# A recurrent weighted average in chunks: v cast to bf16 by its load, constant matrices built on another engine, and the last steps of the state placed anew

## The chip, the cores and the metric

The kernel runs on one core of one Trainium2 chip. The metric is the device time of one execution in microseconds. The names of the engines are those of the profile: PE is the matmul engine, DVE the vector engine, ACT the scalar engine (exponentials, logarithms), POOL the GpSimd engine, SP the engine that issues transfers. POOL and SP both have a queue of transfers between HBM and the on-chip memory (SBUF); all transfers run on the same 16 DMA engines.

## The reference

`k` and `v` are 16 sequences of 2048 steps with 256 channels, `w` and `u` one vector of 256 each, all f32. Each sequence and channel keeps a weighted sum of v (`aa`) and of weights (`bb`), with a running exponent `pp` that keeps the exponentials in range:

```python
for t in range(seq_len):
    ww = u + kk                       # kk, vv: row t of k and v
    qq = np.maximum(pp, ww)
    e1, e2 = np.exp(pp - qq), np.exp(ww - qq)
    output[b, t] = (e1 * aa + e2 * vv) / (e1 * bb + e2 + 1e-08)
    ww = pp - w + kk
    qq = np.maximum(ww, kk)
    e1, e2 = np.exp(ww - qq), np.exp(kk - qq)
    aa, bb, pp = e1 * aa + e2 * vv, e1 * bb + e2, qq
```

## The kernel before, in words

Time is cut into a head of 32 steps and 16 steps of time of 126 rows each. Rows of time lie on the 128 partitions. For one step of time the 16 sequences are taken four at a time, which gives four *pairs* (two tiles of two sequences, 512 columns each). With two pairs for the heads there are 66 pairs, and the main loop runs over them by number `n`, with a tail of 12 rounds (`for n in range(NP + LAG + 2)`).

A pair goes through these steps; line numbers are those of the profile before.

- `load(n)`, four pairs ahead (`AHEAD = 4`): one transfer of k and one of v, 512 KB each, both f32 (L135; for the heads L129). The first two pairs and the heads' k are issued by SP, everything else by POOL.
- `round_k(n)` (L285, DVE): k into the type the matmul reads.
- `logs(n)` (L301, PE): two constant matrices turn k into the exponents of the weights, in PSUM.
- `exps(n)` (L315, L317, ACT): the exponentials, bf16, into the buffer `ez`.
- `cast_v(n)` (L328 on DVE; L326 on ACT for pairs 2 to 7): v into bf16, buffer `vb`.
- `times_v(n)` (L336, DVE): the weights times v, bf16, also into `ez`.
- `sums(n)` (L366, PE): sums over time for the state.
- ten rounds later (`LAG = 10`; six for the heads): `den` (L512, PE) the denominators, `log_den` and `invert` (L521, L526, ACT) their reciprocals as exp of minus the logarithm, `num` (L534, PE) the numerators, `mult` (L542, DVE) the product, and `store` (L562; heads L553), issued by POOL.

Once per step of time a chain of small operations carries the state: `copy_sums`, `turn_sums` (L382), `split_sums` (L389), the state's logarithms and weights (L401 to L421), `state_sums` to `state_decay` (L439 to L450), `inject_logs`, `inject_weights` (L455, L461), `carry_weights`, `carries` (L466, L473), `turn_carries` (L479) and `inject` (L484), whose four small transfers on SP (L488) put the carried state as two more rows into `ez`, where `den` and `num` read them.

Nothing is left to a scheduler: a helper `K` pins every engine's instructions to the order in which the program writes them. The small operations are put into slots of the main loop by tables (`PLANS`): an entry such as `(2, "d3", state_offset, 0)` means the slot `d3` of the round two after the step's last pair. There are plans for the head, the first step, all steady steps and the last.

The constant matrices that `den` and `num` read (`Id`, `IdN`, `It`, `Lh`, `LhN`, `Lf`, `LfN`) are built by POOL in rounds 3, 4 and 5 (L253 to L273), between its transfers.

Of the kernel before, what the change touches and what calls it, by code (L numbers as in the profile page):

```python
# [7 lines left out]
F32 = mybir.dt.float32  # L8
# [14 lines left out]
def kernel(  # L23
# [28 lines left out]
    HS = 63  # L52
# [7 lines left out]
    AHEAD = 4  # L60
    LAG = 10
    HALVES = 8

    SHARED = range(2, HALVES)
    RS = 2.0 ** -43
    LNRS = 43 * 0.6931471805599453
    CAP = 68.0
# [2 lines left out]
    consts = ctx.enter_context(tc.tile_pool(name="consts", bufs=1))  # L70
    kpool = ctx.enter_context(tc.tile_pool(name="kpool", bufs=AHEAD))
    vpool = ctx.enter_context(tc.tile_pool(name="vpool", bufs=AHEAD))
    vbpool = ctx.enter_context(tc.tile_pool(name="vbpool", bufs=2))
# [25 lines left out]
    def is_head(n):  # L99
        return pairs[n][0] < 0  # L100
# [5 lines left out]
    def tiles_of(n):  # L106
        return 1 if pairs[n] == (-1, 1) else 2
# [5 lines left out]

    def load(n):
        kr = kpool.tile([128, 4, Dm], F32, tag="kr", name="kr")
        vr = vpool.tile([128, 4, Dm], F32, tag="vr", name="vr")
        kr_of[n], vr_of[n] = kr, vr
        c, p = pairs[n]
        if is_head(n):
            if p == 1:  # L120
                K(POOL.memset(kr[64:96, 0:2, :], 0.0))
                K(POOL.memset(vr[64:96, 0:2, :], 0.0))

            for t, x, eng, groups in ((kr, k, SP, range(NG)), (vr, v, POOL, reversed(range(NG)))):
                for g in groups:
                    b = 6 * g + 4 * p
                    e = min(b + 2 * tiles_of(n), B)
                    if b < e:
                        K(eng.dma_start(out=t[g * GB:(g + 1) * GB, 0:e - b, :],  # L129
                                        in_=x[b:e, 0:T0, :].rearrange("n t d -> t n d")))  # L130
        else:
            t0 = T0 + c * TC
            r = min(128, T - t0)
            for t, x in ((kr, k), (vr, v)):
                K((SP if n < 2 else POOL).dma_start(  # L135
                    out=t[0:r, :, :], in_=x[4 * p:4 * p + 4, t0:t0 + r, :].rearrange("n t d -> t n d")))


    crow = consts.tile([128, Dm], F32, tag="crow", name="crow")
# [12 lines left out]
    def matrix(name, dt, width=128):  # L152
        return consts.tile([128, width], dt, tag=name, name=name)
# [3 lines left out]
    def select(ap, cmp, fill, base, cm, n, step):  # L157
        K(POOL.affine_select(out=ap, in_=ap, pattern=[[step, n]], compare_op=cmp,
                             fill=fill, base=base, channel_multiplier=cm))
# [21 lines left out]
    K(POOL.memset(cc[:, 5:6], CAP - LNRS))  # L181
    select(cc[:, 4:5], GE, 0.0, -HS, 1, 1, 0)
    select(cc[:, 4:5], GE, 0.0, TC - 1, -1, 1, 0)

    def head_blocks(f):
        fill(f[0:GB, GB:NH], 0.0)
# [63 lines left out]

    def matrices_for_outputs():

        K(POOL.tensor_copy(It, I1))  # L253
        K(POOL.tensor_copy(Id, I1))
        K(POOL.tensor_copy(Id[:, TC:128], I1[:, TC - 1:TC].broadcast_to([128, 128 - TC])))
        K(POOL.tensor_scalar(IdN, Id, RS, None, ALU.mult))

    def matrices_for_outputs_of_head():
        for t, s in ((Lh, 1.0), (LhN, RS)):
            K(POOL.tensor_scalar(t, M1, -s, None, ALU.mult))  # L260
            K(POOL.memset(t[0:GB, GB:NH], 0.0))
            K(POOL.memset(t[GB:2 * GB, 2 * GB:NH], 0.0))
            K(POOL.memset(t[:, NH:128], 0.0))

    def more_matrices_for_outputs():
        Lx = matrix("Lx", F32)
        K(POOL.tensor_scalar(Lx, M1, -1.0, None, ALU.mult))
        K(POOL.memset(Lx[0:HS, HS:TC], 0.0))
        K(POOL.tensor_scalar(Lx[:, 0:HS], Lx[:, 0:HS], cc[:, 2:3], None, ALU.add))
        K(POOL.tensor_scalar(Lx[:, HS:TC], Lx[:, HS:TC], cc[:, 3:4], None, ALU.add))  # L270
        K(POOL.tensor_copy(Lx[:, TC:128], Lx[:, TC - 1:TC].broadcast_to([128, 128 - TC])))
        K(POOL.tensor_copy(Lf, Lx))
        K(POOL.tensor_scalar(LfN, Lx, RS, None, ALU.mult))  # L273


    EZ, X_of, KM = {}, {}, {}
# [39 lines left out]
        else:  # L316
            K(SC.activation(ez_of(n)[:, 0:4:2], X[2][:, :, 0:i, :], ACT.Exp))  # L317

    VB = {}

    def cast_v(n):
        r = NH if is_head(n) else TC
        i = 2 * tiles_of(n)
        vb = vbpool.tile([128, 4, Dm], BF16, tag="vb", name="vb")
        if n in SHARED:
            K(SC.activation(vb[0:r, 0:i, :], vr_of.pop(n)[0:r, 0:i, :], ACT.Copy))  # L326
        else:
            K(DVE.tensor_copy(vb[0:r, 0:i, :], vr_of.pop(n)[0:r, 0:i, :]))  # L328
        VB[n] = vb

    def times_v(n):
        ez = ez_of(n)
        i = tiles_of(n)
        r = NH if is_head(n) else TC
        vb = VB.pop(n).rearrange("p (i n) d -> p i (n d)", i=2)
        K(DVE.tensor_mul(ez[0:r, 1:4:2], ez[0:r, 0:4:2],  # L336
                         vb[0:r, 0:i, :].unsqueeze(1).broadcast_to([r, 2, i, D])))

# [205 lines left out]
    def store(n):  # L544
        o = RD.pop(n).rearrange("p i (n d) -> p (i n) d", n=2)
        if n % 2 == 1:
            EZ.pop(n // 2)
        if is_head(n):
            for g in range(NG):
                b = 6 * g + 4 * pairs[n][1]  # L550
                e = min(b + 2 * tiles_of(n), B)
                if b < e:
                    K(POOL.dma_start(out=out[b:e, 0:T0, :].rearrange("n t d -> t n d"),  # L553
                                     in_=o[g * GB:(g + 1) * GB, 0:e - b, :]))
        else:
            c, p = pairs[n]
            t0 = T0 + c * TC


            r = rows_of(n)  # L560
            for a, b, eng in ((0, 2, POOL), (2, 4, SP)) if n == NP - 1 else ((0, 4, POOL),):
                K(eng.dma_start(out=out[4 * p + a:4 * p + b, t0:t0 + r, :].rearrange("n t d -> t n d"),  # L562
                                 in_=o[0:r, a:b, :]))

# [9 lines left out]
    def small_work(n, where):  # L574
        for f, args in later.pop((n, where), []):
# [14 lines left out]
                   (3, "d4", state_decay, 0), (4, "a0", inject_logs), (4, "a2", inject_weights),  # L590
                   (4, "d4", carry_weights), (4, "d5", carries), (4, "p4", turn_carries), (5, "d0", inject),
                   (5, "d2", state_add, 1), (5, "d4", state_decay, 1)),
        "last": ((1, "a0", copy_sums), (1, "p1", turn_sums), (1, "p1", split_sums), (1, "a2", state_logs),
                 (1, "d5", state_offset, 0), (1, "d5", state_offset, 1), (1, "d5", state_near),
                 (1, "a1", state_weights), (2, "d0", state_sums), (2, "d0", state_add, 0),
                 (2, "d0", state_decay, 0), (2, "a2", inject_logs), (2, "a2", inject_weights),
                 (2, "d2", carry_weights), (2, "d2", carries), (2, "p2", turn_carries), (2, "d5", inject)),
    }
    for c in range(-1, NST):
        for slot, where, f, *args in PLANS["head" if c < 0 else "first" if c == 0 else  # L600
                                           "last" if c + 1 == NST else "steady"]:
# [6 lines left out]
    matrices_for_sums()  # L608
    round_k(0)
    logs(0)  # L610
    cast_v(0)

    out_at = {n + (LAG - 4 if is_head(n) else LAG): n for n in range(NP)}
    for n in range(NP + LAG + 2):

        q, qi, qp = out_at.get(n), out_at.get(n - 1), out_at.get(n - 2)
        live, more, out_q, out_qi, out_qp = n < NP, n + 1 < NP, q is not None, qi is not None, qp is not None
        if n == NP:
            widen()
        if n + AHEAD < NP:  # L620
            load(n + AHEAD)
        small_work(n, "a3")
        if live:
            exps(n)
        small_work(n, "d0")
        if more:
            round_k(n + 1)
        small_work(n, "p0")
        if out_qp:
            num(qp, 0)  # L630
            if not live:
                num(qp, 1)
        small_work(n, "d1")
        small_work(n, "a0")
        small_work(n, "p1")
        if out_qi and qi < NP - 1:
            invert(qi)
        small_work(n, "a2")
        if out_q:
            den(q)  # L640
            if q < NP - 1:
                log_den(q)
            else:
                for i in range(2):
                    log_den(q, i, i + 1)
                    invert(q, i, i + 1)
        if out_qp:
            mult(qp, 0)
        small_work(n, "d2")
        if more:  # L650
            cast_v(n + 1)
# [49 lines left out]
```

## Time and profile before

| what | value |
|---|---|
| median of 13 runs | 325.17 us (322.6 to 331.73) |
| the profiled execution's own time | 325.17 us |
| its span in the profile | 323.5 us |
| PE, DVE, ACT busy | 279.4, 277.4, 278.1 us (86% each) |
| POOL busy | 179.4 us (55%) |
| HBM read, written | 68.12 MB, 34.05 MB |

The profile lists, for each engine, when it was busy, and for each idle stretch what ended it. A stage table (stretch in us, busy time of PE, weight loads, DVE, ACT, POOL, granted clock, share of time in which the 16 DMA engines had a packet in work, GB/s) shows where in the span an engine is full. Packets of one DMA engine overlap by a little, so the share can read above 1. In a row of the groups stand the line, the engine, the operation, the shapes, the count, the total and mean duration, and the idle time ahead of it with its cause.

### The profile page before, as it was taken

Reading aid. Unit: us, or ns where it says so; the run is one execution under the profiler, and the core shown is the slowest. Engines: PE = TensorE matmul, PEld = TensorE weight load, DVE = VectorE, ACT = ScalarE, POOL = GpSimd, SP = SyncE. Lnnn points to the kernel's source line nnn. Section 1 sums busy time; section 2 is a strip of 40 time slices with the busy share of each in tenths; the row PEclk is TensorE's granted clock in tenths of the full one; section 3 lists DMA queues with packets and bytes.
Section 4 is the critical chain, followed back from the end, with each engine's and each line's share of the span. In section 5 each row is a group of like instructions: output and inputs, shape, how many; then the busy total and the mean of one; then the engine's idle time right before and its main releaser. Section 6 shows DMA issues by size and latency. Waiting matters only on the chain. (4 is left out here: it accounts for less than half of the span.)

```text
span 323.5 us, 3974 instructions
## 1 busy us (share of the span) xinstructions
PE 279.4 (86%) x1132; PEld 126.0 (39%) x1132; DVE 277.4 (86%) x546; ACT 278.1 (86%) x318; POOL 179.4 (55%) x249
## 2 busy tenths in 40 slices
PE   2589679889999999999999999999999999987970
PEld 1134334344444444444434444443444444433420
DVE  4565887989999999999999999999999999987670
ACT  6468888789899998989898989999898989796990
POOL 8669954673665555666464666555566656122331
PEclk9999999999999999999999999999999999999995
DMA  6999699999999999999999999999999999944875
GB/s 199 224 326 300 201 316 317 320 324 337 331 353 335 364 375 370 358 367 366 360 356 365 370 361 367 359 364 354 365 370 358 357 317 295 302 177 135 295 253 166
DMA packets 33743, 102.96 MB, mean 318 GB/s; under 512 B 6638, under 2 KB 9482, under 8 KB 33722
## 3 DMA queue, kind: packets, MB, share of 16 engines
q0 software_dynamic: 27616, 99.27, 90.0%
q1 hardware_dynamic: 6074, 3.42, 4.4%
q8 instruction: 9, 0.15, 0.2%
q14 instruction: 12, 0.10, 0.1%
q10 hardware_dynamic: 32, 0.02, 0.1%
HBM read 68.12 MB, written 34.05 MB: 316 GB/s over the span
## 5 line engine op out<-in xcount | busy, mean ns | idle before, releaser
L562 POOL DMA_DIRECT2D out_dram<-rd x64 | 53.7, 840 | 120.5 <-issue 43.0
L317 ACT ACTIVATE ez<-X 128x2048 bf16<-128x2048 f32 x58 | 108.7, 1873 | 8.2 <-PE num L534 6.3
L542 DVE TENSOR_TENSOR rd<-num,rd 128x512 f32<-128x512 f32 (+2 forms) x131 | 88.8, 684 | 14.1 <-ACT rd L526 6.7
L336 DVE TENSOR_TENSOR ez<-ez,vb 126x2048 bf16<-126x2048 bf16 (+1 forms) x66 | 79.7, 1207 | 7.2 <-ACT ez L315 6.8
L521 ACT ACTIVATE rd<-den 128x1024 f32<-128x1024 f32 (+3 forms) x67 | 66.9, 998 | 15.4 <-PE den L512 13.4
L526 ACT ACTIVATE rd<-rd 128x1024 f32<-128x1024 f32 (+3 forms) x67 | 69.4, 1035 | 0.3
L301 PE MATMUL X<-km,NLE 128*128 128x512 f32 x128 | 52.3, 490 | 11.0 <-DVE km L285 8.6
L135 POOL DMA_DIRECT2D kr<-in_k_dram x62 | 56.1, 905 | 2.8 <-DVE kmh L285 1.6
L534 PE MATMUL num<-ez,LfN 128*128 128x512 bf16 x128 | 49.1, 384 | 4.4 <-DVE rd L542 0.8
L135 POOL DMA_DIRECT2D vr<-in_v_dram x62 | 48.6, 784 | 4.7 <-DVE ez L336 2.9
L534 PE MATMUL num<-ez,IdN 126*128 126x512 bf16 (+1 forms) x131 | 49.8, 380 | 0.0
L328 DVE CAST vb<-vr 126x1024 bf16<-126x1024 f32 x60 | 46.3, 772 | 1.0 <-DMA vr<-in_v_dram 1.0
L285 DVE CAST km<-kr 126x1024 fp32r<-126x1024 f32 x64 | 44.2, 691 | 2.8 <-ACT ez L315 1.9
L366 PE MATMUL tot<-ez,OHV 126*48 126x512 bf16 x128 | 38.9, 385 | 8.7 <-DVE ez L336 7.3
L301 PE MATMUL X<-km,NLZ 128*128 128x512 f32 x128 | 41.4, 405 | 0.3 <-ACT ez L315 0.2
L366 PE MATMUL tot<-ez,OHE 128*48 128x512 bf16 x128 | 40.1, 396 | 0.0
L512 PE MATMUL den<-ez,Lf 128*128 128x512 bf16 x128 | 38.0, 378 | 2.1 <-DMA ez<-row 1.3
L512 PE MATMUL den<-ez,Id 126*128 126x512 bf16 (+1 forms) x131 | 39.1, 378 | 0.0
L301 PEld LDWEIGHTS X<-km,NLE 128*128 128x128 f32 x128 | 23.9, 194 | 23.7 <-DVE km L285 6.5
L301 PEld LDWEIGHTS X<-km,NLZ 128*128 128x128 f32 x128 | 24.7, 194 | 6.8 <-ACT ez L315 1.2
L366 PEld LDWEIGHTS <-OHV 126*48 126x48 bf16 x128 | 13.4, 104 | 31.2 <-issue 22.3
L534 PEld LDWEIGHTS <-LfN 128*128 128x128 bf16 x128 | 12.3, 96 | 28.6 <-issue 25.4
(111 smaller groups left out, 215.8 us busy)
## 6 DMA issues: line engine op xcount, KB each, us to landing
out_dram<-rd POOLq DMA_DIRECT2D x60, 512.0 KB, 7.2
kr<-in_k_dram POOLq DMA_DIRECT2D x58, 512.0 KB, 8.1
vr<-in_v_dram POOLq DMA_DIRECT2D x58, 512.0 KB, 8.6
kr<-in_k_dram POOLq DMA_DIRECT2D x4, 504.0 KB, 11.2
vr<-in_v_dram POOLq DMA_DIRECT2D x4, 504.0 KB, 12.1
out_dram<-rd POOLq DMA_DIRECT2D x3, 504.0 KB, 4.4
kr<-in_k_dram SPq DMA_DIRECT2D x2, 512.0 KB, 5.4
vr<-in_v_dram SPq DMA_DIRECT2D x2, 512.0 KB, 9.5
```

Of the source, the lines that this page charges most:

```text
L135: K((SP if n < 2 else POOL).dma_start(out=t[0:r, :, :], in_=x[4 * p:4 * p + 4, t0:t0 + r, :].rearrange("n t d -> t n d")))
L301: K(PE.matmul(X[q][:, i, :], m[0:kr, :], km[0:kr, i, :], start=True, stop=True))
L317: K(SC.activation(ez_of(n)[:, 0:4:2], X[2][:, :, 0:i, :], ACT.Exp))
L328: K(DVE.tensor_copy(vb[0:r, 0:i, :], vr_of.pop(n)[0:r, 0:i, :]))
L336: K(DVE.tensor_mul(ez[0:r, 1:4:2], ez[0:r, 0:4:2], vb[0:r, 0:i, :].unsqueeze(1).broadcast_to([r, 2, i, D])))
L366: K(PE.matmul(TOT[c], m[0:r, :], ez_of(n)[0:r, q, i, :], start=n == first_of[c] and i == 0 and q == 0, stop=n == last_of[c] and i == tiles ...
L512: K(PE.matmul(d[:, i, :], m[0:r, :], ez_of(n)[0:r, q, i, :], start=q == 0, stop=q == 2, skip_group_check=True))
L521: K(SC.activation(RD[n][0:r, a:b, :], DEN[n][0:r, a:b, :], ACT.Ln, scale=RS))
L526: K(SC.activation(RD[n][0:r, a:b, :], RD[n][0:r, a:b, :], ACT.Exp, scale=-1.0))
L534: K(PE.matmul(d, m[0:r, :], ez_of(n)[0:r, q, i, :], start=q == 1, stop=q == 3, skip_group_check=True))
L542: K(DVE.tensor_mul(RD[n][0:r, i, :], NUM.pop((n, i))[0:r, :], RD[n][0:r, i, :]))
L562: K(eng.dma_start(out=out[4 * p + a:4 * p + b, t0:t0 + r, :].rearrange("n t d -> t n d"), in_=o[0:r, a:b, :]))
```

## The change

Five things are edited.

1. v is loaded into a bf16 buffer, so the transfer casts; `cast_v` and the buffer `vb` are gone, and `times_v` reads the loaded buffer. POOL issues all of these loads: the first two pairs' v loads move from SP to POOL, behind the first of POOL's constants. The heads' v groups are issued in rising order.
2. The output matrices are built by DVE, in the same slots, with `LhN` and `LfN` made from `Lh` and `Lf`.
3. The state chain of the last step but one gets a plan of its own, `"before"`: most of its entries stand between a few slots and a whole round earlier than in the steady plan. The chain of the last step has some entries in other slots.
4. In the tail, one pair's second numerator is issued a little later, and one pair's denominators a round earlier, ahead of the last carries.
5. The last store but one is issued by SP.

```diff
-        vr = vpool.tile([128, 4, Dm], F32, tag="vr", name="vr")
+        vr = vpool.tile([128, 4, Dm], BF16, tag="vr", name="vr")
...
-            for t, x, eng, groups in ((kr, k, SP, range(NG)), (vr, v, POOL, reversed(range(NG)))):
-                for g in groups:
+            for t, x, eng in ((kr, k, SP), (vr, v, POOL)):
+                for g in range(NG):
...
-            for t, x in ((kr, k), (vr, v)):
-                K((SP if n < 2 else POOL).dma_start(
-                    out=t[0:r, :, :], in_=x[4 * p:4 * p + 4, t0:t0 + r, :].rearrange("n t d -> t n d")))
+            K((SP if n < 2 else POOL).dma_start(
+                out=kr[0:r, :, :], in_=k[4 * p:4 * p + 4, t0:t0 + r, :].rearrange("n t d -> t n d")))
+            if n >= 2:
+                load_v(n)
+
+    def load_v(n):
...
+        K(POOL.dma_start(out=vr_of[n][0:r, :, :],
+                         in_=v[4 * p:4 * p + 4, t0:t0 + r, :].rearrange("n t d -> t n d")))
...
     select(cc[:, 4:5], GE, 0.0, TC - 1, -1, 1, 0)
+    for n in range(2):
+        load_v(n)
...
-        K(POOL.tensor_copy(It, I1))
-        K(POOL.tensor_copy(Id, I1))
-        K(POOL.tensor_copy(Id[:, TC:128], I1[:, TC - 1:TC].broadcast_to([128, 128 - TC])))
-        K(POOL.tensor_scalar(IdN, Id, RS, None, ALU.mult))
+        K(DVE.tensor_copy(It, I1))
+        K(DVE.tensor_copy(Id[:, 0:TC], I1[:, 0:TC]))
+        K(DVE.tensor_copy(Id[:, TC:128], I1[:, TC - 1:TC].broadcast_to([128, 128 - TC])))
+        K(DVE.tensor_single_scalar(IdN, Id, RS, op=ALU.mult))
...
-        for t, s in ((Lh, 1.0), (LhN, RS)):
-            K(POOL.tensor_scalar(t, M1, -s, None, ALU.mult))
...
+        K(DVE.tensor_single_scalar(Lh, M1, -1.0, op=ALU.mult))
+        head_blocks(Lh)
+        fill(Lh[:, NH:128], 0.0)
+        K(DVE.tensor_single_scalar(LhN, Lh, RS, op=ALU.mult))
...
-    def cast_v(n):
...
-        vb = VB.pop(n).rearrange("p (i n) d -> p i (n d)", i=2)
+        vb = vr_of.pop(n)[:, 0:2 * i, :].rearrange("p (i n) d -> p i (n d)", n=2)
...
-            for a, b, eng in ((0, 2, POOL), (2, 4, SP)) if n == NP - 1 else ((0, 4, POOL),):
+            for a, b, eng in ((0, 2, POOL), (2, 4, SP)) if n == NP - 1 else ((0, 4, SP if n == NP - 2 else POOL),):
...
+        "before": ((1, "a0", copy_sums), (1, "p2", turn_sums), (1, "d5", split_sums), (2, "a3", state_logs),
+                   (2, "d1", state_offset, 0), (2, "d2", state_offset, 1), (2, "d3", state_near),
+                   (2, "a1", state_weights), (3, "d0", state_sums), (3, "d1", state_add, 0),
+                   (3, "d1", state_decay, 0), (3, "a0", inject_logs), (3, "a2", inject_weights),
+                   (3, "d4", carry_weights), (3, "d5", carries), (3, "p4", turn_carries), (4, "d0", inject),
+                   (4, "d2", state_add, 1), (4, "d4", state_decay, 1)),
...
-                 (1, "d5", state_offset, 0), (1, "d5", state_offset, 1), (1, "d5", state_near),
+                 (1, "d2", state_offset, 0), (1, "d2", state_offset, 1), (1, "d2", state_near),
...
-                 (2, "d2", carry_weights), (2, "d2", carries), (2, "p2", turn_carries), (2, "d5", inject)),
+                 (2, "d5", carry_weights), (2, "d5", carries), (2, "a1", turn_carries), (2, "a1", inject)),
...
-            if not live:
+            if n > NP:
                 num(qp, 1)
...
+        if n == NP:
+            num(qp, 1)
...
-            den(q)
+            if q not in DEN:
+                den(q)
+            if n == NP + 1:
+                den(q + 1)
```

More of the change, by code (lines that the diff above doesn't have):

```diff
@@ L62 @@
     HALVES = 8
-    SHARED = range(2, HALVES)
     RS = 2.0 ** -43
@@ L72 @@
     vpool = ctx.enter_context(tc.tile_pool(name="vpool", bufs=AHEAD))
-    vbpool = ctx.enter_context(tc.tile_pool(name="vbpool", bufs=2))
     ezpool = ctx.enter_context(tc.tile_pool(name="ezpool", bufs=7))
@@ L133, in load @@
             r = min(128, T - t0)
-            for t, x in ((kr, k), (vr, v)):
-                K((SP if n < 2 else POOL).dma_start(
-                    out=t[0:r, :, :], in_=x[4 * p:4 * p + 4, t0:t0 + r, :].rearrange("n t d -> t n d")))
+            K((SP if n < 2 else POOL).dma_start(
[3 more added lines that the diff above has]
+    def load_v(n):
+        c, p = pairs[n]
+        t0 = T0 + c * TC
+        r = min(128, T - t0)
+        K(POOL.dma_start(out=vr_of[n][0:r, :, :],
+                         in_=v[4 * p:4 * p + 4, t0:t0 + r, :].rearrange("n t d -> t n d")))
     crow = consts.tile([128, Dm], F32, tag="crow", name="crow")
@@ L251, in matrices_for_outputs @@
     def matrices_for_outputs():
-        K(POOL.tensor_copy(It, I1))
-        K(POOL.tensor_copy(Id, I1))
-        K(POOL.tensor_copy(Id[:, TC:128], I1[:, TC - 1:TC].broadcast_to([128, 128 - TC])))
-        K(POOL.tensor_scalar(IdN, Id, RS, None, ALU.mult))
+        K(DVE.tensor_copy(It, I1))
+        K(DVE.tensor_copy(Id[:, 0:TC], I1[:, 0:TC]))
+        K(DVE.tensor_copy(Id[:, TC:128], I1[:, TC - 1:TC].broadcast_to([128, 128 - TC])))
+        K(DVE.tensor_single_scalar(IdN, Id, RS, op=ALU.mult))
     def matrices_for_outputs_of_head():
-        for t, s in ((Lh, 1.0), (LhN, RS)):
[L260 to L263, printed above, removed]
-    def more_matrices_for_outputs():
[L266 to L273, printed above, removed]
+        K(DVE.tensor_single_scalar(Lh, M1, -1.0, op=ALU.mult))
+        head_blocks(Lh)
+        fill(Lh[:, NH:128], 0.0)
+        K(DVE.tensor_single_scalar(LhN, Lh, RS, op=ALU.mult))
+    def more_matrices_for_outputs():
+        K(DVE.tensor_single_scalar(Lf, M1, -1.0, op=ALU.mult))
+        fill(Lf[0:HS, HS:TC], 0.0)
+        K(DVE.tensor_scalar(Lf[:, 0:HS], Lf[:, 0:HS], cc[:, 2:3], None, ALU.add))
+        K(DVE.tensor_scalar(Lf[:, HS:TC], Lf[:, HS:TC], cc[:, 3:4], None, ALU.add))
+        K(DVE.tensor_copy(Lf[:, TC:128], Lf[:, TC - 1:TC].broadcast_to([128, 128 - TC])))
+        K(DVE.tensor_single_scalar(LfN, Lf, RS, op=ALU.mult))
     EZ, X_of, KM = {}, {}, {}
@@ L317, in exps @@
             K(SC.activation(ez_of(n)[:, 0:4:2], X[2][:, :, 0:i, :], ACT.Exp))
-    VB = {}
-    def cast_v(n):
[L322 to L329, printed above, removed]
     def times_v(n):
@@ L334, in times_v @@
         r = NH if is_head(n) else TC
-        vb = VB.pop(n).rearrange("p (i n) d -> p i (n d)", i=2)
+        vb = vr_of.pop(n)[:, 0:2 * i, :].rearrange("p (i n) d -> p i (n d)", n=2)
         K(DVE.tensor_mul(ez[0:r, 1:4:2], ez[0:r, 0:4:2],
-                         vb[0:r, 0:i, :].unsqueeze(1).broadcast_to([r, 2, i, D])))
+                         vb[0:r].unsqueeze(1).broadcast_to([r, 2, i, D])))
     TOT, SUMS = {}, {}
@@ L600 @@
         for slot, where, f, *args in PLANS["head" if c < 0 else "first" if c == 0 else
-                                           "last" if c + 1 == NST else "steady"]:
+                                           "last" if c + 1 == NST else "before" if c + 2 == NST else "steady"]:
             at(last_of[c] + slot, where, f, c, *args)
@@ L610 @@
     logs(0)
-    cast_v(0)
     out_at = {n + (LAG - 4 if is_head(n) else LAG): n for n in range(NP)}
@@ L649 @@
         small_work(n, "d2")
-        if more:
-            cast_v(n + 1)
         small_work(n, "d3")
```

## The prediction

> **What bounds the kernel now.** I read the first part of the page, then the busy time by stage, the waits of each engine inside the steady stretch, and last the account of the DMA queues.
>
> ```profile
> span 323.5 us, 3974 instructions
> PE 279.4 (86%) x1132; PEld 126.0 (39%) x1132; DVE 277.4 (86%) x546; ACT 278.1 (86%) x318; POOL 179.4 (55%) x249
> ...
> 20.00:30.00 10.00, 10.00 (x29) 4.15 (x27) 5.32 (x7) 7.66 (x11) 8.07 (x15) 1.00 1.03 348
> 30.00:40.00 10.00, 7.38 (x28) 3.17 (x27) 8.00 (x17) 8.89 (x16) 9.41 (x15) 1.00 0.62 190
> 40.00:50.00 10.00, 7.75 (x33) 3.46 (x32) 8.50 (x14) 7.99 (x9) 4.78 (x6) 1.00 1.03 320
> 50.00:60.00 10.00, 9.05 (x38) 4.01 (x37) 8.03 (x16) 9.50 (x10) 6.52 (x9) 1.00 0.97 295
> 60.00:100.00 40.00, 36.59 (x152) 16.88 (x152) 37.23 (x73) 35.13 (x41) 22.65 (x27) 1.00 1.00 341
> 100.00:260.00 160.00, 150.66 (x632) 68.71 (x631) 153.73 (x295) 148.27 (x166) 93.08 (x110) 1.00 1.02 362
> ```
>
> The columns after the stretch are PE, weight loads, DVE, ACT, POOL, then the granted clock, the DMA engines' busy share and GB/s. Three engines tie at 86% over the span. From 100 to 260 us DVE is the fullest, 153.73 of 160 us (96%), PE has 94% and ACT 93%. The last but one column is as important: 1.02. The packets of one DMA engine overlap a little, so "always busy" is not 1.00; where loads alone queue up (20 to 30 us) it reads 1.03. So beside a DVE at 96% stand DMA engines at about 1.02 / 1.03 = 99%.
>
> ```profile
> 149.45 1.88 ACT L317 ACTIVATE ez<-X 128x2048 bf16<-128x2048 f32 x1 [0.24 <-PE num L534]
> 166.88 1.88 ACT L317 ACTIVATE ez<-X 128x2048 bf16<-128x2048 f32 x1 [0.22 <-PE num L534]
> ...
> DVE row L484 <- PE den L479: 3.9, 12, 0.3
> PE tot L366 <- DVE ez L336: 5.0, 13, 0.8
> ACT rd L521 <- PE den L512: 9.0, 12, 1.4
> ```
>
> Between those two exponentials lies one step of time of four pairs: 17.43 us, 4.36 us a pair. The three waits are the longest of DVE, PE and ACT from 60 to 260 us (total, times, longest): all on each other, none on a load. So an in-order round of the compute engines sets the pace, DVE first in it, and the DMA engines just keep up, with no slack to speak of.
>
> **The change, part by part.**
>
> *The casts of v.* They go from DVE and ACT.
>
> ```profile
> L328 DVE CAST vb<-vr 126x1024 bf16<-126x1024 f32 x60 | 46.3, 772 | 1.0 <-DMA vr<-in_v_dram 1.0
> 60.00:260.00 200.00, 36.28 (x46) 1.00 1.02 358
> L326 ACT ACTIVATE vb<-vr 126x1024 bf16<-126x1024 f32 x4 | 4.2, 1057 | 0.0
> ```
>
> The middle row is L328 alone: 36.28 / 46 = 0.79 us a pair, 3.16 us a step. DVE would fall from 16.75 us a step (153.73 / 160 x 17.43) to 13.6. The next floors are PE, 150.66 / 160 x 17.43 = 16.4 us, and ACT, 16.2 us. If nothing else bound, a step would take about 16.4 us, 1.0 less. The DMA engines come first: at 1.03 in place of 1.02 a step takes 17.43 x 1.02 / 1.03 = 17.26 us. So most of what DVE gives up becomes idle time of DVE, if a casting load costs the DMA engines what a plain one does.
>
> *The price of a casting load* is the open question: no run shows one. It reads the same f32 bytes from HBM and writes half as many into SBUF. What 16 engines charge for a plain megabyte (queue, kind: packets, MB, share of 16 engines):
>
> ```profile
> q0 software_dynamic: 764, 2.79, 103.0%
> ...
> q0 software_dynamic: 796, 2.92, 84.4%
> ...
> q0 software_dynamic: 3950, 14.39, 100.0%
> ...
> q0 software_dynamic: 1556, 5.27, 102.1%
> ```
>
> These are the stretches 22 to 30 us (loads alone), 302 to 312 (stores alone), 140 to 180 (the steady mix) and 262 to 280. Share x length x 16 / MB gives 47.3, 46.2, 44.5 and 55.8 engine-us per MB. A load (512 KB, 0.524 MB) is then 0.524 x 44.5 / 16 = 1.46 us of all engines, three transfers 4.37 us: the pair's 4.36 again. Loads and stores alone cost nearly the same, so I find no sign that the write into SBUF is dearer than the read, and take an unchanged price, 44.5. Lower end: priced by the bytes written, half of it. Upper end: the dearest row, 55.8, and beyond it two passes, 89. The v loads are 64 x 0.524 + 0.45 = 34 MB, so each engine-us per MB is worth 34 / 16 = 2.1 us of run time while the DMA engines are full.
>
> The Trainium skill, page "Collectives: The Full Stack", Part 3 (why ReduceScatter is half of AllGather), says that the ALU inside a DMA engine adds no cycles and that the number of reads sets the rate; by it the price would be the unchanged one. No run here shows it yet. Its page "DMA: Bandwidth & Descriptors", section Bandwidth, speaks against any steady gain: HBM gives a core about 358 GB/s. By that, 12 x 0.524 MB take 17.6 us a step, no less than now, and the sum below would lose its 2.7 us and end near 320. The row below is this case's answer.
>
> ```profile
> 108.00:120.00 12.00, 11.16 (x48) 4.95 (x46) 11.53 (x23) 11.76 (x15) 7.88 (x9) 1.00 1.03 377
> ```
>
> 377 GB/s over 12 us lies above that limit, so I keep 1.03 as the mark.
>
> *The steady sum.* Filling 1.00 and 1.02 up to 1.03 is worth 40 x 0.03 / 1.03 + 160 x 0.01 / 1.03 = 2.7 us. From 262 to 280 us one queue alone takes 102.1%, so nothing is to be had there.
>
> *The new wait.* The v buffer is now freed by the product (L336), not the cast, and POOL's load of v four pairs on waits for it.
>
> ```profile
> 152.87 0.83 POOL L135 DMA_DIRECT2D vr<-in_v_dram  x1
> 153.32 1.21 DVE L336 TENSOR_TENSOR ez<-ez,vb 126x2048 bf16<-126x2048 bf16 x1
> 154.58 0.68 DVE L542 TENSOR_TENSOR rd<-num,rd 128x512 f32<-128x512 f32 x1
> 155.83 0.77 POOL L562 DMA_DIRECT2D out_dram<-rd  x1 [2.13 <-ACT ez L317]
> ```
>
> The load moves from 152.87 to about 154.53. Behind it on POOL is the store, which needs the product at 154.58 to 155.26 anyway and was issued at 155.83; a load of about 0.8 us fits before that, at most 0.2 us late, and the consumer also moved from the cast to L336. Price 0, bound 0.2 us a pair where POOL is late, nothing while stores are not awaited.
>
> *Constants from POOL to DVE.*
>
> ```profile
> 27.49 2.02 POOL L260 TENSOR_SCALAR LhN<-M 128x128 bf16<-128x128 f32 x1
> ...
> 31.23 0.75 POOL L135 DMA_DIRECT2D vr<-in_v_dram  x1
> 32.01 0.97 POOL L267 TENSOR_SCALAR Lx<-M 128x128 f32<-128x128 f32 x1
> ...
> 36.06 0.53 POOL L273 TENSOR_SCALAR LfN<-Lx 128x128 bf16<-128x128 f32 x1
> 36.55 1.01 POOL L135 DMA_DIRECT2D kr<-in_k_dram  x1
> ...
> L484 DVE CAST row<-den 128x128 bf16<-128x128 f32 x15 | 4.4, 291 | 4.5 <-PE den L479 4.5
> ```
>
> Between 32.0 and 36.6 us POOL builds Lx, Lf and LfN while loads queue behind; the DMA share of 30 to 40 us is 0.62. That hole is 10 x 0.41 / 1.03 = 4.0 us of DMA time, and 50 to 60 us holds another 0.6. On DVE there are 15 instructions, at most 0.29 us each by the L484 row: 4.4 us as an upper bound, beside 10 - 5.32 + 10 - 8.00 = 6.7 us of idle DVE from 20 to 40 us. Cost 0 while that cover lasts, 4.4 us without it. ACT loses its casts of 1.06 us each between the early exponentials, so these follow each other sooner and buffers free earlier. Since a load also waits for its buffer, I count 3.6 of the 4.6 us; the ends are 0 and 4.6.
>
> *The start.* The first two v loads leave SP and follow POOL's first constants; the heads' k loads move up on SP, POOL's later loads move back by two issues.
>
> ```profile
> 2.36 0.51 SPq L135 DMA_DIRECT2D vr<-in_v_dram  x1
> 2.71 0.89 POOL L158 TENSOR_SCALAR_AFFINE_SELECT cc<-cc 128x1 f32<-128x1 f32 x4
> ...
> 12.99 0.69 DVE L328 CAST vb<-vr 126x1024 bf16<-126x1024 f32 x1 [0.26 <-DMA vr<-in_v_dram]
> 13.60 1.22 DVE L336 TENSOR_TENSOR ez<-ez,vb 126x2048 bf16<-126x2048 bf16 x1
> ...
> 16.59 0.69 DVE L285 CAST kmh<-kr 96x1024 fp32r<-96x1024 f32 x1 [1.77 <-DMA kr<-in_k_dram]
> ```
>
> The issue moves from 2.36 to 3.60 at the earliest. The first product ran only at 13.60, behind the cast of the second v at 12.99; that order is gone. At 16.59 DVE waits for a head's k, which now has two 0.51 us issues fewer ahead of it on SP (1.0 us), while POOL's loads 2 and 3 come 1.5 us later (two issues at 0.75). I take 0, ends -1.5 and +1.5.
>
> *The tail.* ACT's waits after 283 us:
>
> ```profile
> ACT rd L521 <- PE den L512: 1.1, 2, 0.7
> ACT lf L401 <- DVE tsum L389: 0.9, 1, 0.9
> ACT w L420 <- DVE near L410: 0.6, 1, 0.6
> ACT rd L521 <- DMA out_dram<-rd: 0.4, 1, 0.4
> ```
>
> 3.0 us idle, the rest of the tail is logarithm and exponential back to back on ACT. The plan that starts the last but one chain a pair earlier, the last chain's new places and the denominators ahead of the carries work on these; I count half, 1.5 us, ends +1 (a chain misplaced) and -3.0. The last but one store on SP leaves POOL's queue: 0.
>
> **Sum.** -2.7 - 3.6 + 0 - 1.5 = -7.8 us. The profiled execution took 325.17 us, 1.7 beside its span, and is itself the median of the 13 runs. 325.2 - 7.8 = 317.4: I say 317.5.
>
> **The rivals.**
>
> *The compute floor.* If the cast makes the load cheaper, priced by bytes written, the DMA engines drop to five sixths and PE's 16.4 us a step binds: 1.0 us for each of the 12.6 steps from 42 to 262 us, 12.6 in place of 2.7. 325.2 - 12.6 - 3.6 - 1.5 = 307.5. For it: DVE's 96% and the waits among compute engines. Against it: the near equal loads and stores above.
>
> *The casting load is dearer: slower.* The DMA engines become the bound with less throughput, every k and v load comes late and DVE waits for them. The gain of 7.8 us is used up at 7.8 / 2.1 = 3.7 engine-us per MB, a price of 48.2 (8% more); from about 49 on the kernel is slower. At 55.8 it is 11.3 x 2.1 = 24 us: 317.5 + 24 = 341. At two passes, 44.5 x 2.1 = 93: 411. For it: DMA at 99% leaves no cover at all. Against it: the read side, which is unchanged.
>
> *Nothing gained in the end.* A price some 3 to 8% higher, 46 to 48, the spread of the plain rows themselves, takes the gain back: 321 to 326.
>
> **How the numbers follow.** The forecast (unchanged price, 312 to 321) has 0.54, the compute floor 0.13, the small surcharge 0.08, the dearer load 0.25, of which half lies beyond 341. The range 304 to 341 leaves out that half, and a little below the floor. About 0.5% (1.6 us) is what these runs can tell from no change. Faster takes the forecast, the floor, and a little of the surcharge, less the forecast's bad ends: 0.66. Same 0.09, slower 0.25.
>
> **What would show it.** Right: in the steady stretch a DMA share of 1.03 to 1.04, DVE near 80%, waits of DVE or PE on loads of k or v where there were none, steps near 17.2 us; no hole between 30 and 40 us; DVE with the constants but no later exponentials from 20 to 40. The engine-us per MB read of the steady stretch gives the cast's price directly. Wrong: a share well under 1 with PE or ACT at 97% (the floor), or a share of 1.03 with fewer GB/s than now and long waits on loads (the dearer load).

## The result, and the profile after

| | median | runs |
|---|---|---|
| before | 325.03 us (320.46 to 331.73) | 48 |
| after | 300.34 us (298.1 to 301.71) | 11 |

The ratio is 0.9266, 95% interval 0.9237 to 0.9295: 24.7 us less. The direction was forecast; the time lies below the range. The profile shown is that of a second set of runs of the changed kernel (median 299.86, ratio 0.9286, 0.9205 to 0.9368; this execution took 299.33 us), because in the first profiled execution (303.99 us) the granted PE clock was low between 10 and 30 us (0.73 and 0.59).

The first part of the page after, and the stages:

```profile
span 297.6 us, 3932 instructions
...
PE 269.4 (91%) x1115; PEld 124.1 (42%) x1132; DVE 247.8 (83%) x501; ACT 269.9 (91%) x312; POOL 161.6 (54%) x231
...
20.00:30.00 10.00, 8.00 (x34) 3.97 (x32) 8.29 (x21) 6.69 (x12) 6.27 (x8) 1.00 1.20 286
30.00:40.00 10.00, 6.99 (x28) 3.28 (x27) 6.84 (x17) 8.11 (x10) 4.15 (x5) 1.00 1.03 242
...
60.00:100.00 40.00, 39.23 (x169) 18.61 (x172) 35.43 (x69) 39.64 (x46) 21.75 (x28) 1.00 1.17 311
100.00:240.00 140.00, 138.97 (x594) 65.02 (x602) 128.10 (x243) 138.60 (x158) 81.77 (x105) 1.00 1.17 329
```

From 100 to 240 us PE and ACT are busy 99% of the time (138.97 and 138.60 of 140), DVE 91.5%. The last but one column, the share of the DMA engines, reads 1.17: more than the 1.03 that the prediction took for full; why the two can't be compared is said under the tell-tales below. The same stretch of before:

```profile
100.00:240.00 140.00, 132.11 (x555) 60.58 (x554) 134.43 (x259) 129.56 (x146) 81.85 (x97) 1.00 1.02 363
```

The exponentials of pairs 25 and 57, eight steps of time apart, first after, then before:

```profile
98.93 1.88 ACT L322 ACTIVATE ez<-X 128x2048 bf16<-128x2048 f32 x1
...
227.57 1.88 ACT L322 ACTIVATE ez<-X 128x2048 bf16<-128x2048 f32 x1
```

```profile
110.20 1.87 ACT L317 ACTIVATE ez<-X 128x2048 bf16<-128x2048 f32 x1
...
249.77 1.88 ACT L317 ACTIVATE ez<-X 128x2048 bf16<-128x2048 f32 x1
```

A step takes (227.57 - 98.93) / 8 = 16.08 us, against (249.77 - 110.20) / 8 = 17.45 us. All steps below are taken between these two pairs. Split at the exponentials of pairs 13 and 60, the span falls by 7.0 us before pair 13 (58.38 to 51.38), by 16.8 between them (205.02 to 188.18) and by 2.0 after pair 60 (60.06 to 58.05).

The longest waits of DVE and ACT, and of POOL, from 60 to 240 us (total, times, longest):

```profile
POOL vr L140 <- DVE AB L443: 27.0, 22, 1.8
POOL vr L140 <- DVE S L399: 24.6, 11, 3.0
...
DVE S L399 <- ACT lf L394: 6.8, 12, 1.1
...
ACT ez L322 <- PE num L527: 1.4, 5, 0.3
...
DVE rd L535 <- DMA vr<-in_v_dram: 0.5, 2, 0.2
```

The first two are the new wait: POOL's load of v stands until a buffer is free, up to 3.0 us. (The profile names the small DVE operation that ends just behind the product `times_v`; it is the product that frees the buffer, as nearly all of these issues start 0.29 to 0.31 us behind the end of a product, and with more buffers the wait goes, as shown below.) Yet the compute engines hardly wait for a load (0.5 us in 180).

### The profile page after: what moved, and what is told of

The parts are those of the page before. It is cut to its first block, busy times and chain, and to the rows that moved or that the text cites. A ratio compares the mean times of both kernels' runs of the same rounds, so it can differ in the third digit from the quotient of the medians.

```text
span 302.3 us, 3949 instructions
## 1 busy us (share of the span) xinstructions
PE 273.9 (91%) x1132; PEld 125.2 (41%) x1132; DVE 247.7 (82%) x501; ACT 270.2 (89%) x312; POOL 161.5 (53%) x231
## 2 busy tenths in 40 slices
DMA packets 58485, 85.94 MB, mean 284 GB/s; under 512 B 6834, under 2 KB 42406, under 8 KB 58464
## 3 DMA queue, kind: packets, MB, share of 16 engines
q0 software_dynamic: 52896, 82.78, 101.5%
## 5 line engine op out<-in xcount | busy, mean ns | idle before, releaser
L140 POOL DMA_DIRECT2D vr<-in_v_dram x64 | 50.6, 790 | 85.7 <-DVE AB L443 29.4
L329 DVE TENSOR_TENSOR ez<-ez,vr 126x2048 bf16<-126x2048 bf16 (+1 forms) x66 | 79.8, 1209 | 9.2 <-ACT ez L320 4.2
L555 POOL DMA_DIRECT2D out_dram<-rd x63 | 52.6, 835 | 46.4 <-issue 15.5
L290 DVE CAST km<-kr 126x1024 fp32r<-126x1024 f32 x64 | 50.7, 792 | 2.0 <-DMA kr<-in_k_dram 2.0
L130 POOL DMA_DIRECT2D kr<-in_k_dram x62 | 47.6, 768 | 0.4 <-issue 0.2
L320 ACT ACTIVATE ez<-X 128x1024 bf16<-128x1024 f32 (+1 forms) x16 | 14.6, 966 | 9.4 <-PE X L306 9.4
## 6 DMA issues: line engine op xcount, KB each, us to landing
kr<-in_k_dram POOLq DMA_DIRECT2D x4, 504.0 KB, 10.7
```

Source lines behind the costliest of these rows:

```text
L140: K(POOL.dma_start(out=vr_of[n][0:r, :, :], in_=v[4 * p:4 * p + 4, t0:t0 + r, :].rearrange("n t d -> t n d")))
L290: K(DVE.tensor_copy(KM[n][0:r, 0:i, :], kr_of.pop(n)[0:r, 0:i, :]))
L329: K(DVE.tensor_mul(ez[0:r, 1:4:2], ez[0:r, 0:4:2], vb[0:r].unsqueeze(1).broadcast_to([r, 2, i, D])))
```

## The experiments

"Step" is the time of one step between pairs 25 and 57. Each ratio is against runs of before on the same chip. The seven runs of before beside the first four experiments lie high (median 328.56 us, against 325.03 for all 48), so those four ratios may read about 1% too low; the steps are read from traces.

**Which part of the change does it?** The changed kernel with plain f32 loads of v and the old casts on DVE and ACT; the constants, the plans and the tail stay as changed:

```diff
-        vr = vpool.tile([128, 4, Dm], BF16, tag="vr", name="vr")
+        vr = vpool.tile([128, 4, Dm], F32, tag="vr", name="vr")
...
+            K(DVE.tensor_copy(vb[0:r, 0:i, :], vr_of.pop(n)[0:r, 0:i, :]))
```

> The changed kernel with v loaded as plain f32 again and cast on DVE (ACT for pairs 2 to 7) as before; constants on DVE, plans and tail stay changed. Theory A (the round of the compute engines with DVE as its fullest was the bound, the DMA engines had slack): steady steps back at 17.4 us, time 319 to 323, so the other edits are worth 2 to 6 us. Theory B (the DMA engines, full with plain loads, held the steps near 17.3 and the casting load freed them): the same 17.4 us steps and 319 to 323. It sizes what is not the cast.

Measured: 321.99 us, ratio 0.9814 (0.974 to 0.9889), step 17.46. And the reverse, the kernel before with the casting load alone (POOL issues the loads of v, as in the change):

```diff
-        vr = vpool.tile([128, 4, Dm], F32, tag="vr", name="vr")
+        vr = vpool.tile([128, 4, Dm], BF16, tag="vr", name="vr")
...
-    def cast_v(n):
```

> The kernel before with the casting load alone: no cast on DVE or ACT, constants still built by POOL, old plans and tail. Both theories: steps near 16.1 us, 12.6 steps x 1.3 = 17 us from the steady part; time 303 to 308. If it came out above 312, the constants or the plans would be what lets the gain through.

Measured: 300.17 us, ratio 0.9167 (0.9087 to 0.9246), step 16.07: less than the 303 to 308 that was expected. The casting load is the whole effect, as far as these runs can tell. The other edits bring 1.9% while the loads are plain (0.9% against all 48 runs of before), none of it in the step, and nothing that shows on top of the cast. The stage row from 100 to 240 us, plain v, then cast alone:

```profile
100.00:240.00 140.00, 131.69 (x547) 60.46 (x555) 134.45 (x258) 129.50 (x145) 81.61 (x97) 1.00 1.02 363
```

```profile
100.00:240.00 140.00, 139.04 (x595) 65.17 (x602) 128.86 (x245) 138.60 (x156) 82.17 (x106) 1.00 1.17 328
```

The first is the row of before over again, the second that of after.

**Is it the freed DVE or the cheaper transfer?** The cast does two things, so each is done alone. First DVE is freed and the load stays plain. The product reads a buffer of ones in place of v, and one column of v is copied into it, 0.15 us a pair, which waits for the load and gives its buffer back; but for that column v takes no part in the result:

```diff
+        K(DVE.tensor_copy(one[0:r, 0, 0:1], vr_of.pop(n)[0:r, 0, 0:1]))
+        vb = one[:, 0:2 * i, :].rearrange("p (i n) d -> p i (n d)", n=2)
```

> The changed kernel, but v is loaded as plain f32 (512 KB a pair) and never cast: the product multiplies by a constant of ones in bf16 in place of v, after a copy of one column of v into it, which waits for the load and frees its buffer. DVE work as in the changed kernel plus about 0.15 us a pair, DMA work as before. Theory A: steps stay near 16.1 to 16.3, time 299 to 304. Theory B: the full DMA engines hold the steps at 17.2 or more, 12.6 x 1.1 = 14 us more, time 312 to 317.

Measured: 317.06 us, ratio 0.967 (0.96 to 0.9739). The stage row, the two exponentials and two of the waits from 60 to 240 us:

```profile
100.00:240.00 140.00, 135.90 (x562) 60.82 (x570) 124.77 (x266) 133.08 (x150) 75.35 (x99) 1.00 1.03 376
```

```profile
104.32 1.87 ACT L324 ACTIVATE ez<-X 128x2048 bf16<-128x2048 f32 x1
...
240.52 1.87 ACT L324 ACTIVATE ez<-X 128x2048 bf16<-128x2048 f32 x1
```

```profile
ACT rd L517 <- DMA out_dram<-rd: 6.3, 13, 0.8
...
DVE km L292 <- DMA kr<-in_k_dram: 0.7, 4, 0.2
```

A step of 17.02 us at a share of 1.03, with ACT waiting for stores (6.3 us, where the kernel before shows no such wait in this stretch): this is the wall that the prediction saw, and the freed DVE runs into it. Then the transfer alone is changed: the casting load stays, and DVE casts k a second time, into a buffer that nobody reads, from pair 8 on:

```diff
+            spare_cast(n + 1)
...
+        K(DVE.tensor_copy(vb[0:TC], kr_spare.pop(n)[0:TC]))
```

> The changed kernel with the casting load, plus a spare cast on DVE in the old place: 126x1024 f32 to bf16 from the k buffer into a buffer that nothing reads, for pairs 8 to 65 (0.79 us each). DMA work as changed, DVE work as before. Theory A: steps back to 17.2 to 17.4, time 315 to 318. Theory B: the DMA engines are relieved, only DVE's own 16.8 us of work a step binds, time 307 to 310.

Measured: 321.34 us (three runs), ratio 0.9813 (0.9735 to 0.9891), slower than either theory had it. A fourth execution took 1442 us, its matmuls over four times as long as usual (the numerators' 1.6 to 1.7 us, against 0.38) at a granted clock of 1.00; it is left out, and what slowed it is not known. The profile is from a repeat:

> The changed kernel with the spare cast on DVE once more, for a profile: time near 322, steps of 17.4 us, DVE at 95 to 96% of the steady stretch, no waits on loads.

Measured: 321.29 us in one run.

```profile
100.00:240.00 140.00, 127.88 (x533) 58.95 (x541) 137.18 (x252) 129.01 (x143) 76.29 (x96) 1.00 1.12 297
```

```profile
103.28 1.88 ACT L324 ACTIVATE ez<-X 128x2048 bf16<-128x2048 f32 x1
...
246.08 1.87 ACT L324 ACTIVATE ez<-X 128x2048 bf16<-128x2048 f32 x1
```

A step of 17.85 us, DVE at 98%, and no engine waits for a load. DVE has more work here than before, 98% of 17.85 against 96% of 17.45, or 0.7 us a step (a reason is given with the six buffers below). So 17.85 is an upper end for the casting load with DVE's old work. The four steps side by side:

| step, us | DVE casts | DVE does not cast |
|---|---|---|
| plain load | 17.45 (before) | 17.02 |
| casting load | 17.85 | 16.08 (after) |

The freed DVE alone gives 0.4 us a step and the cheaper transfer alone none as measured (about 0.3 if DVE's extra 0.7 is taken off, an estimate), both together 1.4. Two bounds lay side by side: the round through DVE and the transfers. The control, the changed kernel itself, ran beside the experiments that follow:

> The changed kernel as it is, on the same chip as the three beside it, for their comparison and for a profile of it. 298 to 303, steps of 16.1 us.

Measured: the 299.86 us quoted with the result.

**What does a casting load cost the DMA engines?** One more load of v per pair from pair 8 on, plain; and, in another kernel, two more that cast. Nobody reads them:

```diff
+            spare = vbpool.tile([128, 4, Dm], F32, tag="spare", name="spare")
+            K(POOL.dma_start(out=spare[0:r, :, :],
+                             in_=v[4 * p:4 * p + 4, t0:t0 + r, :].rearrange("n t d -> t n d")))
```

```diff
+            for j in range(2):
+                spare = vbpool.tile([128, 4, Dm], BF16, tag=f"spare{j}", name=f"spare{j}")
```

> The changed kernel with one more plain load of v, 512 KB f32, for each pair from 8 on, into a buffer that nothing reads: the DMA engines are made the bound on purpose, to read off prices. A plain transfer costs 1.42 us (17.03 us a step of 12 in the run with plain loads and no cast). Theory C (a casting load is priced by the bytes that it writes, 0.71 us): 3 x 1.42 + 0.71 = 4.97 us a pair, 19.9 a step, time near 353. Theory D (it costs as much as still fits the changed kernel's 4.02 us a pair, 4.02 - 2.84 = 1.18 us, and the DMA engines are full there): 5.44 a pair, 21.8 a step, near 380.

> The changed kernel with two more casting loads of v, 512 KB read and 256 KB written each, for each pair from 8 on, into buffers that nothing reads. Theory C (0.71 us each): 2 x 1.42 + 3 x 0.71 = 4.97 us a pair, 19.9 a step, near 353. Theory D (1.18 us each): 6.38 a pair, 25.5 a step, near 432. With the run beside it this gives the price of a casting load twice.

Measured: 377.53 us (ratio 1.1684, 1.1526 to 1.1841), step 22.08; and 446.0 us (1.3803, 1.363 to 1.3975), step 27.08, the second longer than either theory had it. The stage row of each:

```profile
100.00:240.00 140.00, 111.19 (x435) 47.70 (x440) 93.57 (x178) 103.42 (x115) 77.78 (x102) 0.98 1.14 341
```

```profile
100.00:240.00 140.00, 99.73 (x352) 42.03 (x357) 74.58 (x145) 82.86 (x92) 78.02 (x104) 0.89 1.29 277
```

No engine is near full any more, so the transfers are taken to set these steps. To have the two basic mixes free of compute too, work is left out: for all but the heads' pairs the reciprocal of the denominators and the second half of the matmuls that make denominators and numerators. Once with the casting load, once with the plain load and the ones:

```diff
+        if not is_head(n):
+            return
```

> The changed kernel with less compute, to lay bare what its transfers alone allow: the pairs leave out the exponential of minus the logarithm (ACT, about 0.95 us a pair) and the matmuls with Id and IdN in denominators and numerators (PE, 0.86 us a pair). PE and ACT then need about 3.1 us a pair, DVE 3.4. Theory D (with the casting load the DMA engines are still near full, just under 4.02 us a pair): steps of 15.5 to 16.1, time 292 to 300. Theory C (the casting load is priced by the bytes written and leaves clear slack): DVE binds, steps of 14.0 to 14.8, time 278 to 286.

> The same cut in the run with plain f32 loads of v and a constant of ones in the product. The DMA engines were full there at 17.03 us a step, so both theories: 16.9 to 17.2 a step, time 312 to 318. The difference to the run beside it is the relief by the casting load with the same compute.

Measured: 293.24 us (0.9087, 0.8998 to 0.9177) and 312.28 us (0.9678, 0.9533 to 0.9822). Stage row, exponentials, and waits of ACT and DVE from 100 to 240 us; first the casting load:

```profile
100.00:240.00 140.00, 117.76 (x454) 51.59 (x462) 126.84 (x246) 108.86 (x122) 79.50 (x104) 1.00 1.18 331
```

```profile
95.29 1.87 ACT L322 ACTIVATE ez<-X 128x2048 bf16<-128x2048 f32 x1
...
223.50 1.87 ACT L322 ACTIVATE ez<-X 128x2048 bf16<-128x2048 f32 x1
```

```profile
ACT rd L515 <- DMA out_dram<-rd: 25.5, 30, 2.0
...
DVE km L290 <- DMA kr<-in_k_dram: 7.6, 20, 1.2
```

then the plain one:

```profile
100.00:240.00 140.00, 114.32 (x432) 49.43 (x439) 123.29 (x265) 104.21 (x117) 74.60 (x100) 1.00 1.03 377
```

```profile
99.77 1.87 ACT L324 ACTIVATE ez<-X 128x2048 bf16<-128x2048 f32 x1
...
235.35 1.87 ACT L324 ACTIVATE ez<-X 128x2048 bf16<-128x2048 f32 x1
```

With 21 to 30 us of the 140 us of PE's and ACT's work gone, the steps are 16.03 and 16.95 us, hardly below 16.08 and 17.02: engines wait for stores and loads instead, and a load of k takes 10.5 and 10.7 us from issue to landing, where the kernel after has 8.0. These are the floors that the transfers set. A plain mix is three equal transfers a pair: 16.95 / 4 / 3 = 1.41 us each. With the cast, 16.03 / 4 = 4.01 us a pair, less two plain ones, leaves 1.18 us for the casting load, 36 engine-us per MB read and 16% below a plain one. The extra loads give more: 22.08 / 4 - 3 x 1.41 = 1.29, and (27.08 / 4 - 2 x 1.41) / 3 = 1.32. So the price is 1.18 to 1.32 us (each sum assumes that the prices of unlike transfers add), clearly above the 0.71 of a price by the bytes written.

What it is made of was tried with half a plain load: the cut kernel with v's first 128 columns only, 256 KB read and 256 KB written.

```diff
-        vr = vpool.tile([128, 4, Dm], F32, tag="vr", name="vr")
+        vr = vpool.tile([128, 4, Dm // 2], F32, tag="vr", name="vr")
```

> The cut run with plain loads (no cast, a constant of ones in the product, less work on ACT and PE), but of v only the first 128 of 256 columns are loaded, as plain f32: 256 KB read and 256 KB written a pair, as many bytes as a casting load writes. With whole plain loads the transfers allowed 16.95 us a step, with casting loads 16.02. If the bytes written set the price of the casting load, this run gives 16.0 again. If the bytes read count too, this one is cheaper than the casting load: 14.5 to 15.3 a step, where DVE's own work begins to bind, time 280 to 288.

Measured: 286.83 us (two runs; the fastest of three of before there 322.58), step 15.08.

```profile
100.00:240.00 140.00, 127.17 (x492) 55.72 (x491) 133.85 (x298) 120.31 (x130) 87.07 (x111) 1.00 1.01 347
```

DVE, at 96%, is the bound here, so this gives a ceiling only: 15.08 / 4 - 2 x 1.41 = 0.95 us for half a plain load. It writes what the casting load writes and costs less, so the bytes written alone do not set the price. Another reading fits as well: counted at HBM, the mixes with a cast move 12 x 0.524 / 16.03, 16 x 0.524 / 22.08 and 20 x 0.524 / 27.08 MB per us, which is 392, 380 and 387 GB/s, nearly one rate, against 371 for the plain mix. Whether the rate at HBM or the work in the DMA engines sets the limit stays open.

**Does the new wait cost anything?** Six buffers for v in place of four:

```diff
-    vpool = ctx.enter_context(tc.tile_pool(name="vpool", bufs=AHEAD))
+    vpool = ctx.enter_context(tc.tile_pool(name="vpool", bufs=AHEAD + 2))
```

> The changed kernel with six buffers for v in place of four, so that POOL's load of v no longer waits for the product four pairs back. If that wait (POOL on DVE, some 70 us in total in the profile after) costs nothing, the time is that of the changed kernel within 0.5%; if it holds up k loads and stores behind it at the start, 1 to 3 us less.

Measured: 298.75 us, ratio 0.9244 (0.916 to 0.9329), step 16.06. That is the lowest median of all kernels that compute the whole result, but its ratio is within the interval of the control's: the wait costs about 1 us at most. POOL's loads of v no longer wait. It does change DVE. The casts of k from 100 to 240 us, after, then with six buffers:

```profile
L290 DVE CAST km<-kr 126x1024 fp32r<-126x1024 f32 x35 | 29.0, 828 | 0.0
```

```profile
L290 DVE CAST km<-kr 126x1024 fp32r<-126x1024 f32 x35 | 23.9, 684 | 0.0
```

Held back, POOL's issue of v ends inside the next cast of k. DVE and POOL after:

```profile
152.20 1.15 POOL L555 DMA_DIRECT2D out_dram<-rd  x1 [0.58 <-issue]
152.36 0.68 DVE L290 CAST km<-kr 126x1024 fp32r<-126x1024 f32 x1
...
155.22 0.75 POOL L140 DMA_DIRECT2D vr<-in_v_dram  x1 [1.13 <-DVE AB L443]
155.56 0.90 DVE L290 CAST km<-kr 126x1024 fp32r<-126x1024 f32 x1
```

Overlap alone does not stretch a cast. The one at 152.36 lies wholly under the issue of a store and takes 0.68 us; there the issue is the long one, 1.15 us. The one at 155.56 begins 0.34 us into the issue of a load, which ends inside it, and takes 0.90. From 100 to 240 us 25 casts of k start inside an issue of v and take 0.85 to 0.96 us; the nine others take 0.68. On average it is 828 - 684 = 0.14 us a pair, 0.6 us of DVE a step, which idle DVE absorbs. In the kernel with the idle casts, where DVE is full, the casts of k take 824 ns as well, and the idle ones 869, where the casts of v took 796 in the kernel before; together that is about the 0.7 us named there. It may be why its step is 0.4 us longer than before's, which was not tried.

**Is ACT the bound that is left?** The six-buffer kernel with the copy of the state's sums moved from ACT to DVE:

```diff
-        K(SC.activation(ts, TOT.pop(c), ACT.Copy))
+        K(DVE.tensor_copy(ts, TOT.pop(c)))
```

> The changed kernel with six v buffers, and the copy of the sums out of PSUM (0.58 us a step) on DVE in place of ACT. PE and ACT are both at 99% there. If ACT alone sets the round: steps 0.5 us shorter, 292 to 294. If PE or the transfers bind as well: within 1 us of 298.8. If DVE's order gets in the way: above 300.

Measured: 300.82 us, ratio 0.9316 (0.9285 to 0.9346), step 16.20.

```profile
100.00:240.00 140.00, 138.58 (x589) 62.48 (x597) 129.02 (x252) 134.94 (x149) 82.19 (x105) 1.00 1.17 327
```

ACT falls to 96%, PE stays at 99%, and no time is won. ACT alone is not the bound. Whether PE sets the 16.20 us or the copy's new place in DVE's order does, which the expectation had for a time above 300, this run can't tell.

## Why the prediction was wrong in size

**The step that failed** is the price of a casting load. The prediction took "an unchanged price, 44.5" engine-us per MB, 1.46 us a load, since loads alone and stores alone cost nearly the same per megabyte. Those rows are all of transfers that read as much as they write; they say nothing of one that doesn't. Measured in the kernel's own mix it is 1.18 us (36 engine-us per MB) beside 1.41 for a plain load. The steady term was mis-sized by it: 17.45 - 16.08 = 1.37 us a step and 16.8 us between pairs 13 and 60, where the sum had 2.7. Of the 16.8, 7.6 come with the freed DVE at the plain price already (197.44 us between these pairs) and about 9 with the cheaper load. The Trainium skill's rule that was quoted (page "Collectives: The Full Stack", Part 3: the ALU in a DMA engine adds no cycles, the reads set the rate) is about the sums of a collective. Carried over to this load, its second half does not hold: the same reads at half the writes are cheaper here, 1.18 against 1.41 us. No run here tests its first half.

**The wall was near where it was said to be.** Freed DVE with plain loads is the forecast's own assumption, and its ratio is 0.967 (0.96 to 0.9739), a little below the forecast 317.5 / 325.2 = 0.976 (against all 48 runs of before it is 0.975). That the totals lie so close is in part luck: in its trace pair 13 comes 2.6 us earlier, the stretch to pair 60 is 7.6 us shorter and the rest 3.0 longer, where the sum had 3.6, 2.7 and 1.5 less. The step is 17.02 us; the prediction's mark of 1.03 gave 17.26. Rounding is not the reason: the share of POOL's queue alone, with a digit more, rises from 100.4% to 101.5% and gives 17.26 as well. But at 100.4% it moved 50.40 MB in 140 us and at 101.5% 52.22, so a plain megabyte fell from 44.6 to 43.5 engine-us. The busy share of the DMA engines put the wall too high.

**The rival that came true, the compute floor, was too high.** It was 307.5 us, with PE's 16.4 us a step. That came from PE's busy time while it waited for others; a step of 16.08 was reached at 99%, where PE's busy time is 138.97 / 140 x 16.08 = 15.96 us. The matmuls themselves are as long in both (the numerators' two kinds 385 and 381 ns, before and after); they overlap more. So a busy time that PE shows while it waits overstates the floor, here by 0.4 us a step or 5 us in all. A price a sixth lower was enough, so the rival's condition (priced by bytes written) asked more than was needed: at 16.03 the transfers end just below the compute round.

**The start** gave 7.0 us, not 3.6. With plain loads and all other edits it gave 3.3 (pair 13 at 55.08 us), near the term, and the hole from 30 to 40 us is filled there, with a share of 1.03 and 347 GB/s for 0.62 and 190:

```profile
30.00:40.00 10.00, 8.03 (x30) 3.84 (x29) 7.90 (x19) 6.49 (x11) 4.16 (x5) 0.83 1.03 347
```

The casting load alone, with the constants still on POOL, gave 5.5 (52.86 us), so most of the 7.0 comes with the cast. Each is one execution, and the granted clock dips in some (0.83 in the row above), so the split is rough. In the kernel after, 1.03 with 242 GB/s in that slice is not the full load of its steady stretch, 1.17 with 329. POOL's loads wait in a new way there:

```profile
22.89 0.74 POOL L140 DMA_DIRECT2D vr<-in_v_dram  x1 [1.22 <-DVE Lh L267]
...
25.85 0.74 POOL L140 DMA_DIRECT2D vr<-in_v_dram  x1 [1.39 <-DVE Lf L273]
```

The constants `Lh` and `Lf` are named, but both loads start 0.29 us behind the end of a product (22.60 and 25.56 us), as in the steady stretch (0.31): this is the wait for the product again, not for the constants.

**The tail** gave 2.0 us, for 1.5, and that nearness is in part luck. With all tail edits but plain loads, the stretch after pair 60 is 60.86 us, no shorter than before's 60.06; with the cast alone and the old tail it is 58.78, against 58.05 after. So the casting load brings more of it than the edits that the term was for, by one execution each. ACT's waits behind 261 us, 1.8 us in all where 3.0 were:

```profile
ACT rd L514 <- PE den L505: 0.8, 1, 0.8
ACT rd L514 <- DMA out_dram<-rd: 0.6, 1, 0.6
ACT ts L368 <- PE tot L359: 0.2, 1, 0.2
ACT lf L394 <- DVE tsum L382: 0.2, 1, 0.2
```

**The new wait** cost nothing on the path, as said, though POOL stood up to 3.0 us rather than 0.2 and DVE's casts of k grew.

**The tell-tales.** DVE near 80% and waits on loads belong to the wall; DVE shows 91.5% and no such waits. "The engine-us per MB read of the steady stretch gives the cast's price directly" was wrong: the share reads 1.17 after and 1.29 with three casting loads, so by it the cast would have looked dearer. The page says why it can't be compared:

```profile
DMA packets 58485, 85.94 MB, mean 289 GB/s; under 512 B 6834, under 2 KB 42406, under 8 KB 58464
...
HBM read 68.12 MB, written 34.05 MB: 343 GB/s over the span
```

42406 of 58485 packets are below 2 KB: the casting loads travel as packets of 512 bytes, where the plain ones have 4 KB, and a share from so unlike packets in work side by side doesn't tell what a load costs. The 85.94 MB count what arrives: HBM reads and writes are 102.17 MB together, and half of v's 34 MB is missing.

**The HBM limit** of about 358 GB/s a core was no argument against a gain. The Trainium skill (page "DMA: Bandwidth & Descriptors", section Bandwidth) gives it for both cores of an HBM domain streaming at once, and lists a core alone above it. This kernel runs on one core, and the trace agrees: 12 x 0.524 MB in 16.08 us are 391 GB/s, and the plain mix of the freed DVE shows 376 in its row.

## What to carry to other kernels

Where two resources stand within a few per cent of each other (here DVE's round at 17.45 us and the transfers at 17.02), relieving one shows little of what both bring; look for the edit that relieves both, and price it on both. A price taken from transfers that read and write alike is no price for one that casts; leave it open and give the cheaper end a full share of the range. A floor from the busy time of an engine that still waits for others was too high here, for PE and for the DMA engines.

## What was not expected of the hardware

- A casting load (f32 in HBM to bf16 in SBUF, 512 KB read) costs 1.18 to 1.32 us of the DMA engines in this mix, a plain one 1.41. The transfers' floor with it is 16.03 us a step, 16.95 without.
- The share of busy time of the DMA engines reads 1.17 to 1.29 with such loads and 1.03 with plain ones at their floor. Only shares of like transfers can be compared.
- A cast of k on DVE that starts inside POOL's issue of a load of v takes 0.85 to 0.96 us in place of 0.68. Where a store's issue covers the whole cast, the cast keeps its 0.68 us and the issue takes 1.15. The Trainium skill (page "SBUF — State Buffer", section Terms) speaks of a port pair that DVE and GpSimd lock in turn; the trace agrees that one of the two gives way, but the cast at 155.56 grew by 0.22 us for an overlap of 0.41.
